# Feed-forward gate and up products: hi and lo parts of x side by side as one moving operand of 512 columns

## The chip, the cores and the metric

The kernel runs on one core of one Trainium2 chip. The metric is device time in microseconds (us), from the start to the end of one execution; the lower, the better.

## The reference, cut to what matters

A trunk of two layers (DEPTH = 2) over 256 tokens (S) of 1024 channels (D). Each layer has three token mixers, an output projection, a layer norm, a feed-forward part and a second layer norm. The change touches the first half of the feed-forward part, where `x1` is the result of the first norm:

```python
hidden = silu(einsum('bsd,df->bsf', x1, w_ffn_gate[i])) * einsum('bsd,df->bsf', x1, w_ffn_up[i])
ffn = einsum('bsf,fd->bsd', hidden, w_ffn_down[i])
```

The hidden width f is 2816, so the gate and up matrices are 1024 x 2816 each, per layer, in float32.

## The kernel before, in words

**Products.** Every float32 operand a is split into a high part ah, rounded to the matmul's operand type (fp32r), and a low part al = a - ah. A product a·b is taken as ah·bh + ah·bl + al·bh: three matmuls that add into the same PSUM columns. `mm3` (lines 246 to 250) issues these three, so lines L248, L249 and L250 carry nearly all matmul records. In a record "g<-xh,whi" the tile behind the arrow comes first that is moved through the array, then the one that is loaded into it (the stationary operand).

**Weights.** They come as one stream of pieces of 1 MB (128 x 2048 numbers): `dma_chunk` loads a piece into `raw` (three buffers), `split_chunk` makes `whi` on ScalarE (L206) and `wlo` on VectorE (L207) (three buffers each) and then starts the load of a later piece. Each step of the program ends with `step_end`, which splits one piece. At the time that a piece is used, the two behind it are split already; the split of the third behind it takes the buffers that the piece just used leaves.

**Two shapes of product.** Where the result is wanted with channels on the partitions, `gemm_cols` (L252 to L257) is used: a piece holds 256 output columns of the weights for all of the 8 k tiles; for each half m of 128 columns and each k, 128 x 128 weights are stationary and the 256 tokens of x are moved. That is 2 x 8 x 3 = 48 matmuls of 256 columns for a piece, into the two halves of one PSUM bank. Where tokens are wanted on the partitions (`gemm_tok`, `rows_gemm`), the activations are stationary and 512 columns of the weights are moved.

**Feed-forward.** For each layer, 11 rounds (L858 to L868) of a gate piece and an up piece:

```python
pg, pu = gbank(), gbank()
gemm_cols(use_chunk(), xk, pg)
s = misc([P, 2, S])
A.activation(out=s, in_=pg..., func=AF.Silu)      # L862
step_end()
gemm_cols(use_chunk(), xk, pu)
V.tensor_tensor(out=s, in0=s, in1=pu..., op=ALU.mult)   # L865
split_to(hs[...][:, 0, ...], hs[...][:, 1, ...], s)     # L288, L289
step_end()
```

So both layers use 44 pieces in this stage. Its result `hs` feeds the down projection (`rows_gemm`), whose end feeds the second norm. `xh` and `xl`, the parts of x, are two tiles of [128, 8, 256]. There are eight PSUM banks: four handed out in turn by `gbank`, four by `tbank` (transposes, attention and recurrence; unused in the feed-forward rounds).

**Order.** The instructions are placed on the engines by a scheduler; each engine then runs its own in that order, and waits on semaphores.

Of the kernel before, what the change touches and what calls it, by code (L numbers as in the profile page):

```python
# [15 lines left out]
P = 128  # L16
# [13 lines left out]

# columns of the constants' array
K_DIST = 0
# [46 lines left out]
def trunk(ctx: ExitStack, tc: tile.TileContext, x, p, w_in, pool_w, pool_scale, w_branch_a,  # L79
# [13 lines left out]
    def slot(tag, shape, dt=F32):  # L93
        return sl.tile(shape, dt, tag=tag, name=tag)
# [13 lines left out]
    def gbank():  # L108
        return psg.tile([P, 512], F32, tag="g", name="g")

    def tbank():
        return pst.tile([P, 512], F32, tag="t", name="t")
# [3 lines left out]

# [1 line left out]
    ident = cst.tile([P, P], F32, name="ident")  # L118
# [7 lines left out]

# [1 line left out]
    chunks = []  # L128
# [87 lines left out]

# [1 line left out]
    tasks = []  # L218
# [25 lines left out]

# [1 line left out]
    def mm3(ps, a, b, first, last):  # L246
# [5 lines left out]
    def gemm_cols(w, act, ps, nk=8, m0=0, nm=2):  # L252
        for m in range(nm):
            for k in range(nk):
                ms = slice((m0 + m) * P, (m0 + m + 1) * P)
                mm3(ps[:, m * S:(m + 1) * S], (w[0][:, k, ms], w[1][:, k, ms]),
                    act(k), k == 0, k == nk - 1)  # L257

    def xk(k):
        return xh[:, k, :], xl[:, k, :]  # L260
# [7 lines left out]
    def gemm_tok(ws, act, evac, between):  # L268
        """512 output columns, both tiles of tokens, ws: two pieces of four k tiles."""
        for t in range(2):  # L270
            ps = gbank()
            for k in range(KD):
                w = ws[k // 4]
                mm3(ps, act(k, t), (w[0][:, k % 4, :], w[1][:, k % 4, :]), k == 0, k == KD - 1)
                if t == 0 and k == 5 and between is not None:
                    between()
            evac(t, ps)
# [7 lines left out]
    def split_to(hi, lo, src, scale=None):  # L285
        """hi and lo parts of src (SBUF or PSUM), scaled per partition."""
        if scale is None:
            A.activation(out=hi, in_=src, func=AF.Copy)  # L288
            V.tensor_tensor(out=lo, in0=src, in1=f(hi), op=ALU.subtract)  # L289
        else:  # L290
            A.activation(out=hi, in_=src, func=AF.Copy, scale=scale)
            V.scalar_tensor_tensor(out=lo, in0=src, scalar=scale, in1=f(hi), op0=ALU.mult, op1=ALU.subtract)

# [1 line left out]
    def rsqrt(out, v, n):  # L295
# [16 lines left out]
    def layer_norm(t, gb, ress, then):  # L312
        """ress: per half of the columns (base, scale or None, psum)."""
        st = small([P, 2, 6], "ln_st")
        for hf, (base, scale, ps) in enumerate(ress):
            dst = xt[:, t, 512 * hf:512 * hf + 512]
            if scale is None:
                V.tensor_tensor(out=dst, in0=base, in1=ps, op=ALU.add)
            else:
                V.scalar_tensor_tensor(out=dst, in0=base, scalar=scale, in1=ps, op0=ALU.mult, op1=ALU.add)  # L320
            V.bn_stats(out=st[:, hf, :], in_=dst)  # L321
        mv = small([P, 2], "ln_mv")
        V.bn_aggr(out=mv, in_=st)
        ve = small([P, 1], "ln_ve")
        V.tensor_scalar(out=ve, in0=mv[:, 1:2], scalar1=LN_EPS, scalar2=None, op0=ALU.add)
        r = small([P, 1], "ln_r")
        rsqrt(r, ve, 1)
        for hf in range(2):
            cs = slice(512 * hf, 512 * hf + 512)
            V.scalar_tensor_tensor(out=xt[:, t, cs], in0=xt[:, t, cs], scalar=mv[:, 0:1], in1=gb[:, 0, cs],  # L330
                                   op0=ALU.subtract, op1=ALU.mult)
            V.scalar_tensor_tensor(out=xt[:, t, cs], in0=xt[:, t, cs], scalar=r, in1=gb[:, 1, cs],
                                   op0=ALU.mult, op1=ALU.add)
            then(t, hf)
# [6 lines left out]

# [1 line left out]
    def hgrn_task(l, hp, q, ff, kf, fb, kb, vt, gt, oh, ol):  # L343
# [14 lines left out]
        for d in range(2):  # L358
# [29 lines left out]
            yield 660  # L388
            # totals of the chunks of 32
            u = 31 if fwd else 0  # L390
# [4 lines left out]
            kb_ = range(0, 3) if fwd else range(1, 4)  # L395
            # blocks of 64 stand at 0, 2, 4; the one scaled to its tile's far end beside the middle one
            for L, blks, src, intra, own, far, fac in (
# [14 lines left out]
            V.tensor_tensor(out=t64, in0=tot[:, :, :, 0, :], in1=tot[:, :, :, 1, :], op=ALU.mult)  # L412
            # scaled: fwd queries block 3 by total of 2, keys block 0 by total of 1; bwd mirrored
            for L, lo_side, sc in ((QL, not fwd, 2 if fwd else 1), (KL, fwd, 1 if fwd else 2)):
# [14 lines left out]
            for h in range(2):  # L429
                for t in range(2):  # L430
                    # fwd: queries block 2t+1, keys block 2t; bwd: the other way
                    po = 0 if fwd else 64
                    co = (2 * h + t) * 64
                    PE.matmul(cr[po:po + 64, co:co + 64], lhsT=KL[:, h, 4 * t, :], rhs=QL[:, h, 4 * t, :],  # L434
                              start=True, stop=True)
                qp = QL[:, h, 2:4, :] if fwd else QL[:, h, 1:3, :]
                kp = KL[:, h, 1:3, :] if fwd else KL[:, h, 2:4, :]
                co = (2 * h + d) * P
                PE.matmul(lg[:, co:co + P], lhsT=kp.rearrange("p b u -> p (b u)"),  # L439
                          rhs=qp.rearrange("p b u -> p (b u)"), start=True, stop=True)  # L440
# [53 lines left out]

# [1 line left out]
    def attn_task(j, qs, ks, va, vb, ob):  # L496
# [45 lines left out]

# [1 line left out]
    def pool_task(g, a, mix):  # L544
        # a: [P, 2, 272], the channels' values between zeros
        while busy or any(t[0] == "attn1" for t in tasks):
# [7 lines left out]
        for s in range(g + 1):  # L554
            nxt = work([P, 2, 272])
            sh = 1 if s == 0 else 1 << (s - 1)
            # first step: out[t] = a[t-1] + a[t]; then out[t] = cur[t-sh] + cur[t+sh]
            l2 = lo + sh
            r2 = n if s == 0 else n - sh
            right = 0 if s == 0 else sh  # L560
            V.tensor_tensor(out=nxt[:, :, l2:r2], in0=cur[:, :, l2 - sh:r2 - sh],
                            in1=cur[:, :, l2 + right:r2 + right], op=ALU.add)
            cur, lo, n = nxt, l2, r2
            yield 620
# [14 lines left out]

# [1 line left out]
    xh, xl = slot("xh", [P, KD, S], F32R), slot("xl", [P, KD, S], F32R)  # L581
    load_x(0)
# [51 lines left out]
    for l in range(DEPTH):  # L634
        # token-major operands: the recurrence's values and gate
        vt = slot("s4", [P, 2, D])
# [18 lines left out]
        for hp in range(4):  # L655
# [26 lines left out]
            if hp < 3:  # L682
# [3 lines left out]
                tok_block(xperm, ev)  # L686
        # attention
        ob = slot("s8", [P, 2, 4, S], F32R)
# [28 lines left out]

        # gates and branches
        finish("hgrn")
# [66 lines left out]

        # output projection, first norm
        pT = slot("s7", [P, 2, S])
# [10 lines left out]
        def rows_gemm(n, late, act, base):  # L799
            """all columns of both tiles of tokens; the last pieces go tile by tile."""  # L800
            banks = [[gbank(), gbank()], [gbank(), gbank()]]
# [23 lines left out]

        xh, xl = slot("xh", [P, KD, S], F32R), slot("xl", [P, KD, S], F32R)

# [4 lines left out]

        # per-layer embedding
        pl2 = slot("s6", [P, 2, D])
# [19 lines left out]

        # feed-forward
        hs = [slot(tag, [P, 2, 4, S], F32R) for tag in ("sa", "sb", "s4", "s5", "s8")]
        hs.append(slot("s7", [P, 2, 2, S], F32R))
        for c in range(NF // 2):  # L858
            pg, pu = gbank(), gbank()
            gemm_cols(use_chunk(), xk, pg)  # L860
            s = misc([P, 2, S])
            A.activation(out=s, in_=pg.rearrange("p (m t) -> p m t", t=S), func=AF.Silu)  # L862
            step_end()
            gemm_cols(use_chunk(), xk, pu)
            V.tensor_tensor(out=s, in0=s, in1=pu.rearrange("p (m t) -> p m t", t=S), op=ALU.mult)  # L865
            i = 2 * (c % 2)
            split_to(hs[c // 2][:, 0, i:i + 2, :], hs[c // 2][:, 1, i:i + 2, :], s)
            step_end()  # L868
        gb = load_gb("s6", ln2_g[l], ln2_b[l])
        xh, xl = slot("xh", [P, KD, S], F32R), slot("xl", [P, KD, S], F32R)  # L870
        last = l == DEPTH - 1
# [47 lines left out]
```

## Time and profile before

| | |
|---|---|
| time, median of 3 runs | 1344.53 us (1342.67 to 1344.79) |
| profiled execution, first to last instruction (span) | 1341.4 us; no time of its own is listed for it beside the span |
| TensorE matmul busy | 1317.5 us (98%), 9609 matmuls |
| TensorE weight load busy | 1236.9 us (92%) |
| VectorE busy | 868.7 us (65%) |
| ScalarE busy | 585.9 us (44%) |
| mean DMA rate | 174 GB/s |
| mean granted TensorE clock | 0.997 of full speed |

Matmuls overlap in their records: the duration of one (283 ns for 256 columns) counts from its start to its modelled end, while the next starts much earlier. What a matmul costs in a row of matmuls is therefore the distance from one start to the next, which the timeline shows. PE is TensorE's matmul, PEld its weight load, DVE is VectorE, ACT ScalarE, SP the engine that issues the loads.

### The profile page before, as it was taken

The page shows a single profiled execution, that of the slowest core. Times are in us where ns is not written, and L with a number is a line of the kernel's source. Part 1 is how long each engine was busy: PE and PEld are TensorE (multiplying, and loading weights), DVE is VectorE, ACT ScalarE, POOL GpSimd, SP SyncE. Part 2 cuts the span into 40 slices and gives each one's busy share as a digit, 9 for nine tenths or more (in the row PEclk, how much of TensorE's full clock was granted, in tenths as well). Part 3 has the DMA queues.
Part 4 walks back from the last instruction along what each step waited for, and adds up shares of the span by engine and source line. Part 5 has one row for each costly group of instructions (what it writes and reads, how often), then busy time and mean ns, then how long its engine had stood idle before and what let it go on. Part 6 is the DMA issues. An engine that isn't in the chain of part 4 may idle for free.

```text
span 1341.4 us, 22091 instructions
## 1 busy us (share of the span) xinstructions
PE 1317.5 (98%) x9609; PEld 1236.9 (92%) x9609; DVE 868.7 (65%) x1126; ACT 585.9 (44%) x644; POOL 16.6 (1%) x24
## 2 busy tenths in 40 slices
PE   8999999999999999999989999999999999999997
PEld 6899999999999799998779999999999997999986
DVE  4598888574655765544555999875746558544545
ACT  5444444553444444443334444455534444444431
POOL 0000000000000000000000000000000000000000
PEclk9999999999999999999999999999999999999999
DMA  8654544245556465655356554442455564765551
GB/s 309 200 178 158 178 138 161 93 156 181 176 186 219 158 221 188 189 186 190 127 184 196 179 164 158 158 158 95 159 168 186 188 216 142 239 188 183 179 195 40
DMA packets 180769, 233.56 MB, mean 174 GB/s; under 512 B 3841, under 2 KB 149825, under 8 KB 180673
## 3 DMA queue, kind: packets, MB, share of 16 engines
q1 hardware_dynamic: 178976, 227.44, 51.7%
q10 hardware_dynamic: 1696, 4.72, 1.1%
q8 instruction: 75, 1.23, 0.4%
q14 instruction: 22, 0.17, 0.0%
HBM read 231.10 MB, written 1.05 MB: 173 GB/s over the span
## 4 chain that ended last, share of the span: by engine, by line
PE 93%; DVE 4%; issue 1%; ACT 1%; POOL 1%; DMA 0%; POOLq 0%; DVEq 0%; ACTq 0%
PE g L248 29%; PE g L249 28%; PE g L250 28%; DVE wlo L207 2%; PE t L439 1%; PE t L426 1%; PE t L434 1%; PE t L307 1%; POOL rs_y L297 1%; PE t L523 1%; PE t L463 1%; PE t L464 1%; ACT whi L206 0%; DVE ln_st L321 0%; PE t L503 0%
## 5 line engine op out<-in xcount | busy, mean ns | idle before, releaser
L207 DVE TENSOR_TENSOR wlo<-raw,whi 128x2048 fp32r<-128x2048 f32 (+2 forms) x218 | 489.9, 2248 | 339.7 <-ACT whi L206 339.4
L206 ACT ACTIVATE whi<-raw 128x2048 fp32r<-128x2048 f32 (+2 forms) x218 | 410.0, 1883 | 566.7 <-issue 259.6
L248 PE MATMUL g<-xh,whi 128*128 128x256 f32 x1984 | 564.4, 284 | 0.0
L250 PE MATMUL g<-xh,wlo 128*128 128x256 f32 x1984 | 561.7, 283 | 0.0
L249 PE MATMUL g<-xl,whi 128*128 128x256 f32 x1984 | 561.6, 283 | 0.0
L248 PEld LDWEIGHTS g<-xh,whi 128*128 128x128 f32 x1984 | 380.7, 192 | 0.2
L249 PEld LDWEIGHTS g<-xl,whi 128*128 128x128 f32 x1984 | 380.7, 192 | 0.2
L250 PEld LDWEIGHTS g<-xh,wlo 128*128 128x128 f32 x1984 | 380.6, 192 | 0.0
L248 PE MATMUL g<-whi,xh 128*128 128x512 f32 x288 | 115.1, 400 | 1.2 <-ACT whi L206 1.2
L249 PE MATMUL g<-wlo,xh 128*128 128x512 f32 x288 | 114.6, 398 | 1.4 <-DVE wlo L207 1.4
L250 PE MATMUL g<-whi,xl 128*128 128x512 f32 x288 | 113.3, 395 | 0.0
L249 PEld LDWEIGHTS g<-wlo,xh 128*128 128x128 f32 x288 | 55.6, 193 | 14.1 <-DVE wlo L207 3.1
L248 PEld LDWEIGHTS g<-whi,xh 128*128 128x128 f32 x288 | 55.6, 193 | 13.7 <-ACT whi L206 1.8
L250 PEld LDWEIGHTS g<-whi,xl 128*128 128x128 f32 x288 | 55.4, 192 | 11.5
L248 PE MATMUL g<-s,whi 128*128 128x256 f32 x192 | 54.3, 283 | 0.0
L250 PE MATMUL g<-s,wlo 128*128 128x256 f32 x192 | 54.3, 283 | 0.0
L249 PE MATMUL g<-s,whi 128*128 128x256 f32 x192 | 54.3, 283 | 0.0
L249 PE MATMUL g<-wlo,s 128*128 128x512 f32 x128 | 50.1, 392 | 0.0
L250 PE MATMUL g<-whi,s 128*128 128x512 f32 x128 | 50.1, 391 | 0.0
L248 PE MATMUL g<-whi,s 128*128 128x512 f32 x128 | 49.6, 390 | 0.0
L865 DVE TENSOR_TENSOR m<-m,g 128x512 f32<-128x512 f32 x22 | 15.1, 687 | 36.9 <-PE g L250 36.9
L248 PE MATMUL g<-whi,sa 128*128 128x512 f32 x96 | 37.5, 391 | 0.0
(177 smaller groups left out, 1472.4 us busy)
## 6 DMA issues: line engine op xcount, KB each, us to landing
raw<-in_w_in_dram SPq DMA_DIRECT2D x106, 1024.0 KB, 5.1
raw<-in_w_ffn_gate_dram SPq DMA_DIRECT2D x22, 1024.0 KB, 5.4
raw<-in_w_ffn_up_dram SPq DMA_DIRECT2D x22, 1024.0 KB, 5.4
raw<-in_w_ffn_down_dram SPq DMA_DIRECT2D x22, 1024.0 KB, 4.8
raw<-in_w_branch_c_dram SPq DMA_DIRECT2D x8, 1024.0 KB, 5.0
raw<-in_w_branch_a_dram SPq DMA_DIRECT2D x8, 1024.0 KB, 5.0
raw<-in_w_out_dram SPq DMA_DIRECT2D x8, 1024.0 KB, 4.8
raw<-in_w_ple_gate_dram SPq DMA_DIRECT2D x8, 1024.0 KB, 5.1
```

The costliest lines, as they stand in the source:

```text
L206: A.activation(out=hi[:, ks, :], in_=t[:, ks, :], func=AF.Copy)
L207: V.tensor_tensor(out=lo[:, ks, :], in0=t[:, ks, :], in1=f(hi[:, ks, :]), op=ALU.subtract)
L248: PE.matmul(ps, lhsT=ah, rhs=bh, start=first, stop=False)
L249: PE.matmul(ps, lhsT=ah, rhs=bl, start=False, stop=False)
L250: PE.matmul(ps, lhsT=al, rhs=bh, start=False, stop=last)
L297: G.tensor_tensor(out=y, in0=v, in1=mhalf.to_broadcast([P, n]) if n > 1 else mhalf, op=ALU.pow)
L307: PE.transpose(ps[:, k * P:(k + 1) * P], xt[:, t, (4 * hf + k) * P:(4 * hf + k + 1) * P], ident)
L426: PE.matmul(dg[po:po + 64, co:co + 64], lhsT=KI[:, cs], rhs=QI[:, cs], start=True, stop=True)
L434: PE.matmul(cr[po:po + 64, co:co + 64], lhsT=KL[:, h, 4 * t, :], rhs=QL[:, h, 4 * t, :], start=True, stop=True)
L439: PE.matmul(lg[:, co:co + P], lhsT=kp.rearrange("p b u -> p (b u)"), rhs=qp.rearrange("p b u -> p (b u)"), start=True, stop=True)
L463: PE.matmul(o, lhsT=at[:, 2 * h + t, :], rhs=vt[:, t, hs], start=True, stop=False)
L865: V.tensor_tensor(out=s, in0=s, in1=pu.rearrange("p (m t) -> p m t", t=S), op=ALU.mult)
```

## The change

In the feed-forward rounds, `gemm_cols` is replaced by `gemm_wide`. The tiles `xh` and `xl` become the two halves of one tile `xx` of [128, 8, 2, 256], so that for a k tile hi and lo parts of x lie side by side as 512 columns; `xh` and `xl` stay as names of the halves for all other products. For each half m and each k the weights' high part is loaded once and all 512 columns are moved (this gives whi·xh in columns 0 to 255 of a bank and whi·xl in columns 256 to 511); the weights' low part is loaded and the 256 columns of xh are moved, added into columns 0 to 255. So two matmuls (one of 512 columns, "wide", one of 256, "narrow") stand for three of 256. One bank now holds one half m, so that a piece takes two banks: gate pieces take them from `gbank`, up pieces from `tbank`. `joined` reads them: ScalarE copies the first half of the bank to SBUF, VectorE adds the second half, once for each m. Silu and the product of gate and up then read SBUF.

```diff
+    def gemm_wide(w, ps):
+        for m in range(2):
+            ms = slice(m * P, (m + 1) * P)
+            for k in range(KD):
+                wide = (ps[m], w[0][:, k, ms], xx[:, k].rearrange("p a t -> p (a t)"))
+                narrow = (ps[m][:, 0:S], w[1][:, k, ms], xx[:, k, 0, :])
+                for i, (o, a, b) in enumerate((wide, narrow) if k == 0 else (narrow, wide)):
+                    PE.matmul(o, lhsT=a, rhs=b, start=k == 0 and i == 0, stop=k == KD - 1 and i == 1,
+                              skip_group_check=True)
+
+    def joined(ps, dst):
+        for m in range(2):
+            A.activation(out=dst[:, m, :], in_=ps[m][:, 0:S], func=AF.Copy)
+            V.tensor_tensor(out=dst[:, m, :], in0=dst[:, m, :], in1=ps[m][:, S:2 * S], op=ALU.add)
...
-    xh, xl = slot("xh", [P, KD, S], F32R), slot("xl", [P, KD, S], F32R)
+    xx = slot("xx", [P, KD, 2, S], F32R)
+    xh, xl = xx[:, :, 0, :], xx[:, :, 1, :]
...
         for c in range(NF // 2):
-            pg, pu = gbank(), gbank()
-            gemm_cols(use_chunk(), xk, pg)
-            s = misc([P, 2, S])
-            A.activation(out=s, in_=pg.rearrange("p (m t) -> p m t", t=S), func=AF.Silu)
+            pg, pu = [gbank(), gbank()], [tbank(), tbank()]
+            gemm_wide(use_chunk(), pg)
+            s, u = misc([P, 2, S]), misc([P, 2, S])
+            joined(pg, s)
+            A.activation(out=s, in_=s, func=AF.Silu)
             step_end()
-            gemm_cols(use_chunk(), xk, pu)
-            V.tensor_tensor(out=s, in0=s, in1=pu.rearrange("p (m t) -> p m t", t=S), op=ALU.mult)
+            gemm_wide(use_chunk(), pu)
+            joined(pu, u)
+            V.tensor_tensor(out=s, in0=s, in1=u, op=ALU.mult)
             i = 2 * (c % 2)
             split_to(hs[c // 2][:, 0, i:i + 2, :], hs[c // 2][:, 1, i:i + 2, :], s)
             step_end()
```

In the changed file the matmuls of `gemm_wide` are on L268, the copy and the addition of `joined` on L274 and L275, Silu on L883, the product of gate and up on L887, and the lines 288 and 289 of before are 306 and 307.

TensorE's order at the first gate piece of layer 0, before (g is a PSUM bank; a name in brackets is a semaphore that the instruction waits for):

```order
L248 MATMUL g<-xh,whi 128x256 [waits Activation_49]
L249 MATMUL g<-xl,whi 128x256
L250 MATMUL g<-xh,wlo 128x256 [waits DVE_49]
L248 MATMUL g<-xh,whi 128x256
L249 MATMUL g<-xl,whi 128x256
L250 MATMUL g<-xh,wlo 128x256
```

The same place in the changed kernel:

```order
L268 MATMUL g<-xx,whi 128x512 [waits Activation_49]
L268 MATMUL g<-xx,wlo 128x256 [waits DVE_49]
L268 MATMUL g<-xx,wlo 128x256
L268 MATMUL g<-xx,whi 128x512
L268 MATMUL g<-xx,wlo 128x256
L268 MATMUL g<-xx,whi 128x512
L268 MATMUL g<-xx,wlo 128x256
```

Three narrow matmuls became one wide and one narrow, which alternate from the second k on; outside of the feed-forward rounds the order of TensorE, and that of the other engines and of the loads, is that of before.

ScalarE's order in one round of a gate piece and an up piece (the third round of layer 0), before; `whi` is the split of a later piece, the last row the high part of hidden:

```order
L206 ACTIVATE whi<-raw 128x2048 [waits DMAHW2_49,PE_49,Activation_49]
L862 ACTIVATE m<-g 128x512 [waits PE_49]
L206 ACTIVATE whi<-raw 128x2048 [waits DMAHW3_49,PE_49,Activation_49]
L288 ACTIVATE sb<-m 128x512 [waits DVE_49]
```

The same round in the changed kernel:

```order
L274 ACTIVATE m<-g 128x256 [waits PE_49] x2
L206 ACTIVATE whi<-raw 128x2048 [waits DMAHW2_49,Activation_49]
L883 ACTIVATE m<-m 128x512 [waits DVE_49]
L274 ACTIVATE m<-t 128x256 [waits PE_49,Activation_49]
L274 ACTIVATE m<-t 128x256 [waits PE_49]
L206 ACTIVATE whi<-raw 128x2048 [waits DMAHW3_49,Activation_49]
L306 ACTIVATE sb<-m 128x512 [waits DVE_49]
```

The two copies of a piece's halves now stand ahead of the split of a later piece, and Silu waits for VectorE's additions instead of for TensorE.

VectorE's order from a split to the low part of hidden, in a round of layer 0, before:

```order
L207 TENSOR_TENSOR wlo<-raw,whi 128x2048 [waits DMAHW4_49,PE_49,Activation_49]
L865 TENSOR_TENSOR m<-m,g 128x512 [waits PE_49,Activation_49]
L207 TENSOR_TENSOR wlo<-raw,whi 128x2048 [waits DMAHW5_49,Activation_49]
L289 TENSOR_TENSOR sb<-m,sb 128x512 [waits Activation_49]
```

The same round in the changed kernel:

```order
L275 TENSOR_TENSOR m<-m,g 128x256 [waits Activation_49] x2
L207 TENSOR_TENSOR wlo<-raw,whi 128x2048 [waits DMAHW4_49,Activation_49]
L275 TENSOR_TENSOR m<-m,t 128x256 [waits Activation_49] x2
L887 TENSOR_TENSOR m<-m 128x512 [waits DVE_49]
L207 TENSOR_TENSOR wlo<-raw,whi 128x2048 [waits DMAHW5_49,Activation_49]
L307 TENSOR_TENSOR sb<-m,sb 128x512 [waits Activation_49]
```

Two additions stand ahead of each split, each of which waits for ScalarE's copy.

## Rows read from the trace of the kernel before

**Rows 1.** The page: the chain that ended last, shares of the span by engine.

```profile
PE 93%; DVE 4%; issue 1%; ACT 1%; POOL 1%; DMA 0%; POOLq 0%; DVEq 0%; ACTq 0%
```

**Rows 2.** Busy times by stretch: both feed-forward stages, then a row of wide matmuls.

```profile
core 0: us, PE busy (x) PEld busy (x) DVE busy (x) ACT busy (x) POOL busy (x), PEclk, DMA share, GB/s
480.07:606.78 126.71, 126.71 (x1057) 126.70 (x1056) 66.24 (x45) 54.51 (x45) 0.00 (x0) 1.00 0.60 192
1145.98:1272.70 126.72, 126.72 (x1058) 126.71 (x1056) 66.24 (x45) 54.49 (x45) 0.00 (x0) 1.00 0.60 192
608.17:617.69 9.52, 9.52 (x43) 7.88 (x42) 5.19 (x3) 3.09 (x3) 0.00 (x0) 1.00 0.48 179
```

**Rows 3.** Timeline of PE where the stage begins: start, duration, engine, line, out<-in.

```profile
479.62 0.39 PE L249 MATMUL g<-wlo,xh 128*128 128x512 f32 x1
479.85 0.39 PE L250 MATMUL g<-whi,xl 128*128 128x512 f32 x1
480.07 0.28 PE L248 MATMUL g<-xh,whi 128*128 128x256 f32 x1
480.19 0.28 PE L249 MATMUL g<-xl,whi 128*128 128x256 f32 x1
```

**Rows 4.** Timeline of PE where the stage ends and the down projection begins.

```profile
606.66 0.28 PE L250 MATMUL g<-xh,wlo 128*128 128x256 f32 x1
606.78 0.40 PE L248 MATMUL g<-whi,sa 128*128 128x512 f32 x1
607.02 0.40 PE L249 MATMUL g<-wlo,sa 128*128 128x512 f32 x1
...
608.17 0.39 PE L248 MATMUL g<-whi,sa 128*128 128x512 f32 x1
```

**Rows 5.** Waits of PE: who waited for whom, us in total, times, longest.

```profile
PE t L307 <- DVE x L332: 7.5, 6, 3.5
PE t L307 <- DMA x<-in_x_dram: 3.7, 1, 3.7
PE g L249 <- DVE wlo L207: 1.4, 1, 1.4
```

**Rows 6.** Groups by shape: busy us, mean ns of one, idle time before them.

```profile
L698 ACT ACTIVATE h<-g 128x256 f32<-128x256 f32 x48 | 15.5, 378 | 6.0 <-DVE w L406 6.0
L865 DVE TENSOR_TENSOR m<-m,g 128x512 f32<-128x512 f32 x22 | 15.1, 687 | 36.9 <-PE g L250 36.9
L383 DVE TENSOR_TENSOR w<-h,w 128x256 f32<-128x256 f32 x16 | 6.6, 415 | 3.2 <-PE t L426 3.2
```

**Rows 7.** Timelines of ACT, then DVE, then SP, over the first pieces of the stage.

```profile
485.95 1.92 ACT L206 ACTIVATE whi<-raw 128x2048 fp32r<-128x2048 f32 x1 [3.28 <-PE g L249]
...
487.90 2.29 DVE L207 TENSOR_TENSOR wlo<-raw,whi 128x2048 fp32r<-128x2048 f32 x1 [2.58 <-ACT whi L206]
...
490.22 0.37 SPq L193 DMA_DIRECT2D raw<-in_w_ffn_gate_dram  x1
```

**Rows 8.** The page: DMA issues, KB each, us from issue to landing.

```profile
raw<-in_w_ffn_gate_dram SPq DMA_DIRECT2D x22, 1024.0 KB, 5.4
```

**Rows 9.** Timeline of PE behind the second norm of layer 0, then that stretch's busy times.

```profile
679.25 1.33 PE L307 MATMUL t<-ident,x 128*128 128x128 f32 x8 [3.47 <-DVE x L332]
...
681.19 0.63 PE L249 MATMUL g<-wlo,xh 128*128 128x512 f32 x1
681.62 0.63 PE L248 MATMUL g<-whi,xh 128*128 128x512 f32 x1
...
683.75 0.44 PE L250 MATMUL g<-whi,xl 128*128 128x512 f32 x1
...
680.00:690.00 10.00, 9.98 (x39) 7.96 (x40) 3.65 (x3) 4.72 (x5) 0.00 (x0) 0.83 0.03 10
```

More of the change, by code (lines that the diff above doesn't have):

```diff
@@ L824, in rows_gemm @@
                 step_end()
-        xh, xl = slot("xh", [P, KD, S], F32R), slot("xl", [P, KD, S], F32R)
+        xx = slot("xx", [P, KD, 2, S], F32R)
+        xh, xl = xx[:, :, 0, :], xx[:, :, 1, :]
         def ln1(t, b):
@@ L869, in trunk @@
         gb = load_gb("s6", ln2_g[l], ln2_b[l])
-        xh, xl = slot("xh", [P, KD, S], F32R), slot("xl", [P, KD, S], F32R)
+        xx = slot("xx", [P, KD, 2, S], F32R)
+        xh, xl = xx[:, :, 0, :], xx[:, :, 1, :]
         last = l == DEPTH - 1
```

## The prediction

> **What bounds the kernel now.** I read four views, from the whole to the place. First the chain that ended last [rows 1]: TensorE (PE) holds 93% of it, so a stage in which PE never waits is worth exactly what PE's own work in it shrinks by. Second the waits of PE [rows 5]: what PE waits for are transposes behind a norm (L307), the first load of x, and one or two splits; none of the matmuls of the feed-forward rounds is named as waiting. Third the busy times by stretch [rows 2]: in both feed-forward stages, 126.71 and 126.72 us long, PE is busy for all of it, while VectorE has 66 us of work and ScalarE 54.5. So this stage is PE and nothing else, and the other two have half of it free. Fourth the timeline, for the distance from one matmul's start to the next, which is what a matmul costs in a row of them; its recorded duration of 0.28 us is more than twice that.
>
> Two such distances carry the whole sum. A stage is 22 pieces of 48 narrow matmuls (256 columns), 1056 in all, as the count of weight loads (PEld) says; the count of PE has one or two more that still run in from outside: 126.71 / 1056 = 0.1200 us each [rows 2]. The nearest long run of wide matmuls (512 columns) is the down projection: from 608.17 to 617.69 there are 42 of them, counted by weight loads: 9.52 / 42 = 0.2267 us each [rows 2]. Twice the columns cost 0.1067 us more. If 256 columns cost 0.1067 us, a narrow matmul has 0.1200 - 0.1067 = 0.0133 us that does not depend on its columns, and so has a wide one. I call that the start of a matmul.
>
> **The change, part by part.** *Matmuls.* For each half and each k, three narrow ones (0.3600 us) become one wide and one narrow (0.2267 + 0.1200 = 0.3467). The columns are the same 768; what goes is one start, 0.0133 us. A piece has 2 x 8 such places, both layers have 44 pieces: 704 starts x 0.0133 = 9.4 us, or 4.7 us a stage, which should come down from 126.7 to 122.0. All of it lies on the chain.
>
> The row says 0.0133 us for a start. The Trainium skill, page "TensorE: Matmul & The Clock Gate", section "Back-to-back issue gap", gives N/2.4 + 2.5 ns for a lone stream at full clock, so only 2.5 ns that do not depend on the columns; by it my estimate for the saving would be 704 x 2.5 ns = 1.8 us, which nobody could measure here. By that formula the two distances would be 109 and 216 ns; the trace has 120.0 and 226.7, so here the trace disagrees with the page, and I take the rows.
>
> *Reading the banks.* Each piece gains two copies of 128x256 on ScalarE and two additions of 128x256 on VectorE. The nearest rows: a ScalarE instruction of that shape from PSUM takes 0.378 us (L698); for the addition the ends are 0.415 us (L383, same shape, no PSUM) and half of L865's 0.687, 0.344 us (half the columns, from PSUM) [rows 6]. I take 0.415, since a short instruction is not half of a long one. Silu and the product keep their shape and read SBUF; I leave their price. That makes 22 x 0.76 = 16.6 us more on ScalarE, 54.5 + 16.6 = 71 of 122 us, and 22 x 0.83 = 18.3 us more on VectorE, 66.2 + 18.3 = 84.5 of 122 us. Both stay below the stage's length, so I cost them at nothing; without that cover they would be 17 or 18 us a layer.
>
> *What is queued behind the new instructions.* Each engine runs in order, so the split of a later piece now stands behind the copies. A piece that starts at 480.07 ends 48 x 0.12 later, at 485.83; its split partner (the third piece behind it) begins on ScalarE at 485.95, on VectorE at 487.90, and is done at 490.19 [rows 7], 4.4 us after the piece's end. The copy of the second half puts 0.38 us ahead of it; VectorE's addition runs beside the split on ScalarE and adds nothing. So it is done 4.7 us after the piece's end, and PE wants it only two pieces later, after 2 x 5.55 = 11.1 us: 6.4 us to spare. Silu now waits for VectorE's second addition, but that is done (0.38 + 0.42 us) while ScalarE is still in the split ahead of it. The load that is issued at 490.22 [rows 7], when the split ends, lands after 5.4 us [rows 8], and its own split comes three pieces behind the first, 16.6 us after 485.95, at 502.6 in place of 503.2: 7 us to spare. SP's queue is as before.
>
> *Banks.* A bank is written anew after four pieces (eight halves in eight banks), some 22 us; its readers are done within a piece's length. Nothing. What was held up behind the stage, the down projection, takes other banks than the last piece's and uses the last part of hidden at its very end. Nothing.
>
> *Layout of x.* The split of x behind a norm writes with twice the distance between k tiles, and the other products read the same runs of x as before. Ends: nothing, or a few ns for each of the few writes. Nothing.
>
> **The sum** against the profiled execution: 1341.4 - 9.4 = 1332.0 us of span. The median of the runs is 3.1 us above that span (the lowest run 1.3); I let that distance stand, so 1344.5 - 9.4 = 1335.1 us.
>
> **The rivals.** *A wide matmul behind a narrow one costs more than in a row of its kind.* Where the narrow run ends, the first wide one takes 0.24 us to the next start, and the six from 606.78 to 608.17 take 1.39 us where six of 0.2267 take 1.36 [rows 4]: 0.005 us each. Now every wide one follows a narrow one. With 0.005 on each, 704 x 0.005 = 3.5 us are lost again: 1338.6. Against it stands the other joint: from the last wide start before the stage to the second narrow one are 0.34 us [rows 3] where 0.2267 + 0.1200 are 0.3467, so that the two joints may cancel. Chance 0.09.
>
> *Only that second joint holds*: 0.0067 us less for each pair, 704 x 0.0067 = 4.7 us more gain: 1330.4. Chance 0.04.
>
> *The distance goes by what is loaded, not by the width.* The wide rows that I read have activations loaded and weights moved; in the changed stage it is the other way round, as in the narrow rows. And in the narrow stage the weight load (PEld) is busy for 126.70 of 126.71 us, against 7.88 of 9.52 in the wide stretch [rows 2]. If each column of this stage costs 0.1200 / 256 us whatever the width, a wide one takes 0.24 us and nothing is gained: 1344.5. For it: the load is as full as PE. Against it: both kinds load 128x128, and the two distances differ by 256 columns at one rate. Chance 0.05.
>
> *Slower: each change of width costs the whole settling.* The six wide starts behind the narrow run lose 0.03 us in all [rows 4]. If that is the price of one change of width, and is paid at once each time, 704 x 0.03 = 21.1 us come on, against 9.4 saved: 1356.2. It decides from 0.0133 us a pair on. Against it: the first wide one shows at most 0.0133 of it, and the joint of rows 3 shows no loss. Chance 0.04.
>
> That the change does not do what it says I leave out: the new order of TensorE has one wide and one narrow for every three.
>
> **How the numbers follow.** My forecast, the plain sum, has 0.78. Its own width: the runs lie from 1.9 below to 0.3 above the median; and behind the second norm of layer 0, where PE had waited 3.47 us, the starts of wide ones stand 0.43 us apart, six in 2.56 us from 681.19 to 683.75 [rows 9]. The granted clock there is 0.83 in a stretch of 10 us, which is half speed (1.2 in place of 2.4 GHz) for about 3.4 us, worth 1.7 us. Whether that happens once, twice or not at all may change when the stages shift by 4.7 us. Together 1331.5 to 1337.1; to hold 8 in 10 with the first rival's 1338.6 inside it, 1331.5 to 1339.0. Left out are the fall to 1330.4, no change and slower, 0.13.
>
> A difference of 0.2% (2.7 us) is about what a measurement of this kernel can tell from none. Faster by more: the forecast, the first and the second rival, 0.78 + 0.09 + 0.04 = 0.91. Within it: the third, 0.05. Slower: 0.04.
>
> **What will show it.** Right, if the trace of the changed kernel has 8905 matmuls, both stages at 122.0 us with PE busy throughout, 0.347 us from one wide start to the next, no wait of PE on L268, and VectorE at some 85 us in a stage. If the stage is longer with PE full, it is one of the joints, and the distances behind wide and narrow ones say which. If PE has gaps at L268, the splits or the banks are late and my spare time of 6.4 us was wrong. If the stage has 122 us and the time does not follow, it was given back behind a norm.

## The result and the profile after

The changed kernel takes 1336.74 us (median of 4 runs, 1335.85 to 1337.37), against 1343.68 us before (median of 4 runs, 1342.67 to 1344.79, the three shown above and one more beside the new kernel). The ratio is 0.9948, with a 95% interval from 0.9936 to 0.9960: 0.4% to 0.6% faster. The forecast was 1335.1 us, faster, within 1331.5 to 1339.0; the time lies inside, and 6.9 us were saved where 9.4 were forecast.

The busy times of the changed kernel in both feed-forward stages, and then in a stretch behind the second norm of layer 0 (columns as in [rows 2]):

```profile
480.69:603.73 123.04, 123.04 (x705) 107.21 (x704) 82.43 (x88) 69.04 (x88) 0.00 (x0) 1.00 0.62 197
1143.82:1266.87 123.05, 123.05 (x705) 107.21 (x704) 82.44 (x88) 68.97 (x88) 0.00 (x0) 1.00 0.62 197
676.29:681.64 5.35, 5.35 (x16) 4.34 (x17) 1.90 (x3) 1.20 (x2) 0.00 (x0) 0.50 0.17 64
```

The stages went from 126.71 and 126.72 us [rows 2] to 123.04 and 123.05, 3.67 each, where the forecast said 4.7. PE is busy for all of it, as before. The trace has 8905 matmuls, as forecast. The weight load, whose row had been as full as PE's, now has 16 us free in a stage; but the record of one load lasts 0.19 us, so this row is full wherever loads start closer together than that, and by itself it says little about a limit.

The waits of PE in the changed kernel:

```profile
PE t L325 <- DVE x L350: 7.6, 6, 3.6
PE t L325 <- DMA x<-in_x_dram: 3.7, 1, 3.7
PE g L249 <- DVE wlo L207: 1.4, 1, 1.4
```

They are those of [rows 5], one for one; no matmul of L268 is among them. So nothing holds PE up in the stage: its own matmuls take longer than forecast. Its timeline, in the first half of an up piece, shows where:

```profile
486.74 0.40 PE L268 MATMUL t<-xx,whi 128*128 128x512 f32 x1
486.97 0.28 PE L268 MATMUL t<-xx,wlo 128*128 128x256 f32 x1
487.09 0.40 PE L268 MATMUL t<-xx,whi 128*128 128x512 f32 x1
487.33 0.28 PE L268 MATMUL t<-xx,wlo 128*128 128x256 f32 x1
487.45 0.40 PE L268 MATMUL t<-xx,whi 128*128 128x512 f32 x1
487.69 0.28 PE L268 MATMUL t<-xx,wlo 128*128 128x256 f32 x1
487.80 0.40 PE L268 MATMUL t<-xx,whi 128*128 128x512 f32 x1
```

A wide start is followed after 0.23 to 0.24 us, a narrow one after 0.11 to 0.12. Over the whole stage of layer 0, read to the nanosecond, a wide one takes 233.8 ns on average (7.2 more than 226.7) and a narrow one 115.8 (4.2 less than 120.0). Over a stage, a pair takes 123.05 / 352 = 0.3496 us where 0.2267 + 0.1200 = 0.3467 were forecast. The excess is not even: by the starts in the trace, the eight pairs of the first half of a piece take 352.1 ns each, those of the second half 347.1, in piece after piece.

The new readers, in the groups by shape:

```profile
L275 DVE TENSOR_TENSOR m<-m,g 128x256 f32<-128x256 f32 x44 | 18.4, 418 | 12.4 <-ACT m L274 12.4
L274 ACT ACTIVATE m<-t 128x256 f32<-128x256 f32 x44 | 16.9, 384 | 52.4 <-PE t L268 52.2
```

**Where the span went.** From 1341.4 to 1335.6 us it fell by 5.8 in these two profiled executions. The two stages give 7.3. Two other stretches, whose order of work is the same in both kernels, give some back. The stage of layer 0 begins at 480.69 in place of 480.07, 0.6 us later. From its end to the stage of layer 1 there are 1143.82 - 603.73 = 540.09 us, where there were 1145.98 - 606.78 = 539.20, 0.9 more. The second is the clock behind the norm. In the timeline of the changed kernel, after the wait for the norm:

```profile
676.29 1.94 PE L325 MATMUL t<-ident,x 128*128 128x128 f32 x8 [3.58 <-DVE x L350]
...
678.65 0.63 PE L249 MATMUL g<-wlo,xx 128*128 128x512 f32 x1
...
681.64 0.58 PE L248 MATMUL g<-whi,xx 128*128 128x512 f32 x1
682.06 0.40 PE L249 MATMUL g<-wlo,xx 128*128 128x512 f32 x1
```

The steps of 0.43 us (half speed, 1.2 in place of 2.4 GHz; the row above has a granted clock of 0.50 there) last from 678.65 to 682.06, eight of them, where before there were six, from 681.19 to 683.75 [rows 9], and the transposes ahead of them already take 1.94 us in place of 1.33. This comes with the run and not with the change: the four runs of the changed kernel itself have spans of 1334.1 and 1334.5 us with a mean granted clock of 0.997, and of 1335.4 and 1335.6 with 0.996. Likewise, from the end of one stage to the start of the other there are 539.2 to 539.4 us in the profiled runs of before and of e1, e2, e4 and e9 below, and 539.8 to 540.3 us in those of the changed kernel and of e3, e5, e6, e7 and e11, while the program between the stages does the same in all of them.

The 0.6 us at the start are of the same kind. In the changed kernel, the first products run at half speed up to a start at 12.96:

```profile
12.53 0.63 PE L248 MATMUL g<-whi,xx 128*128 128x512 f32 x1
12.96 0.43 PE L249 MATMUL g<-wlo,xx 128*128 128x512 f32 x1
```

The next start is at 13.23. Before, the last of these steps of 0.43 ended at 11.20. (The windows of the profile list a granted clock of 1.00 for this stretch in both, so here the half speed is read from the steps alone.) In the other kernels below whose part ahead of the stage is the same (all but e8 and e10), the stage of layer 0 begins anywhere from 479.68 to 480.64, so this too comes with the run and not with the change.

### The profile page after: what moved, and what is told of

It reads as the page before. It is cut to its first block, busy times and chain, and to the rows that moved or that the text cites. A ratio compares the mean times of both kernels' runs of the same rounds, so it can differ in the third digit from the quotient of the medians.

```text
span 1335.6 us, 20897 instructions
## 1 busy us (share of the span) xinstructions
PE 1311.6 (98%) x8905; PEld 1199.4 (90%) x8905; DVE 902.0 (68%) x1214; ACT 615.1 (46%) x732; POOL 16.7 (1%) x24
## 4 chain that ended last, share of the span: by engine, by line
PE 93%; DVE 4%; issue 1%; ACT 1%; POOL 1%; DMA 0%; POOLq 0%; DVEq 0%; ACTq 0%
PE g L248 22%; PE g L249 22%; PE g L250 22%; PE t L268 9%; PE g L268 9%; DVE wlo L207 2%; PE t L457 1%; PE t L444 1%; PE t L452 1%; PE t L325 1%; POOL rs_y L315 1%; PE t L541 1%; PE t L481 1%; PE t L482 1%; ACT whi L206 0%
## 5 line engine op out<-in xcount | busy, mean ns | idle before, releaser
L248 PE MATMUL g<-xx,whi 128*128 128x256 f32 x1280 | 365.2, 285 | 0.0
L250 PE MATMUL g<-xx,wlo 128*128 128x256 f32 x1280 | 362.5, 283 | 0.0
L249 PE MATMUL g<-xx,whi 128*128 128x256 f32 x1280 | 362.4, 283 | 0.0
L248 PEld LDWEIGHTS g<-xx,whi 128*128 128x128 f32 x1280 | 245.6, 192 | 0.2
L249 PEld LDWEIGHTS g<-xx,whi 128*128 128x128 f32 x1280 | 245.6, 192 | 0.2
L250 PEld LDWEIGHTS g<-xx,wlo 128*128 128x128 f32 x1280 | 245.5, 192 | 0.0
L268 PE MATMUL t<-xx,whi 128*128 128x512 f32 x352 | 123.6, 396 | 0.0
L268 PE MATMUL g<-xx,whi 128*128 128x512 f32 x352 | 123.6, 396 | 0.0
L248 PE MATMUL g<-whi,xx 128*128 128x512 f32 x288 | 115.7, 402 | 1.2 <-ACT whi L206 1.2
L249 PE MATMUL g<-wlo,xx 128*128 128x512 f32 x288 | 114.8, 398 | 1.4 <-DVE wlo L207 1.4
L250 PE MATMUL g<-whi,xx 128*128 128x512 f32 x288 | 113.6, 396 | 0.0
L268 PE MATMUL g<-xx,wlo 128*128 128x256 f32 x352 | 90.9, 279 | 0.0
L268 PE MATMUL t<-xx,wlo 128*128 128x256 f32 x352 | 90.9, 279 | 0.0
L268 PEld LDWEIGHTS g<-xx,whi 128*128 128x128 f32 x352 | 64.5, 188 | 12.0
L268 PEld LDWEIGHTS t<-xx,whi 128*128 128x128 f32 x352 | 64.5, 188 | 11.9
L268 PEld LDWEIGHTS t<-xx,wlo 128*128 128x128 f32 x352 | 66.3, 188 | 3.9
L268 PEld LDWEIGHTS g<-xx,wlo 128*128 128x128 f32 x352 | 66.3, 188 | 3.9
L248 PEld LDWEIGHTS g<-whi,xx 128*128 128x128 f32 x288 | 55.9, 194 | 13.7 <-ACT whi L206 1.8
L250 PEld LDWEIGHTS g<-whi,xx 128*128 128x128 f32 x288 | 55.6, 193 | 11.7
```

The source lines that it names most:

```text
L248: PE.matmul(ps, lhsT=ah, rhs=bh, start=first, stop=False)
L249: PE.matmul(ps, lhsT=ah, rhs=bl, start=False, stop=False)
L250: PE.matmul(ps, lhsT=al, rhs=bh, start=False, stop=last)
L268: PE.matmul(o, lhsT=a, rhs=b, start=k == 0 and i == 0, stop=k == KD - 1 and i == 1, skip_group_check=True)
```

## The experiments

Eleven kernels ran. The question was why a pair takes 2.9 ns more than the sum of its parts, and whether the readers, the layout, the halves or the banks have a share in it. The stage is compared by its length in the trace, which is the same in both layers to 0.02 us in every kernel; a kernel's single time carries the run's clock with it.

**e1_grouped: in each half the wide ones first, then the narrow ones.**

```diff
-            for k in range(KD):
...
-                for i, (o, a, b) in enumerate((wide, narrow) if k == 0 else (narrow, wide)):
...
+            wide = [(ps[m], w[0][:, k, ms], xx[:, k].rearrange("p a t -> p (a t)")) for k in range(KD)]
+            narrow = [(ps[m][:, 0:S], w[1][:, k, ms], xx[:, k, 0, :]) for k in range(KD)]
+            order = wide + narrow
+            for i, (o, a, b) in enumerate(order):
...
```

> For each half the eight wide matmuls come first, then the eight narrow ones; nothing else differs from the changed kernel, whose feed-forward stage takes 123.05 us (a wide and a narrow one together 349.6 ns on average, 352.0 in the first half of a piece and 347.1 in the second). Theory 'joints' (the step between a wide and a narrow one costs 2.9 ns a pair): with two joints left in a half instead of sixteen, a pair costs 226.7 + 120.0 = 346.7 ns and the stage 122.0 to 122.2 us. Theory 'first half' (something of the first half of a piece, its weights' place, its bank or its time, costs 5 ns a pair): the stage stays at 123.0 us and the first half at 352.

Measured: 1336.06 us (median of 4; ratio to before 0.9948, interval 0.9932 to 0.9965), stage 122.88 us. Its timeline, merged by group:

```profile
490.82 2.00 PE L268 MATMUL g<-xx,whi 128*128 128x512 f32 x8
492.67 1.11 PE L268 MATMUL g<-xx,wlo 128*128 128x256 f32 x8
493.62 2.00 PE L268 MATMUL g<-xx,whi 128*128 128x512 f32 x8
```

Eight wide ones take 1.84 to 1.85 us from first start to the next group, where 8 x 0.2267 = 1.81; eight narrow ones 0.95, where 8 x 0.1200 = 0.96. By the single starts: behind a narrow run, wide ones step by 233, 236, 229, 232, 231 and then 227 ns, 27.7 ns over in all; behind a wide run, narrow ones step by 113, 119 and then 120, 8 ns under. That is 19.7 ns a trip (from narrow to wide and back), or 2.5 ns a pair here. The first half is no longer slower than the second (349.0 and 349.2). Neither expectation met it: the joints do not vanish, because the whole price of a joint is spread over several matmuls, and where the widths alternate the next joint comes before it is paid. A stage of the changed kernel has 308 such trips and is 1.03 us over 352 undisturbed pairs (122.02 us): 3.3 ns a trip. This run has 44, and 0.86 us over: 19.5 ns a trip.

**e2_halves_swapped** (`for m in (1, 0)`), **e3_banks_swapped** (`ps[1 - m]` in place of `ps[m]`, in the products and in the join).

> The loop over the two halves of a piece runs backwards (columns 128 to 255 of the weights first), each with the bank that it had. Theory 'place': the half with columns 0 to 127 costs 352 ns a pair wherever it comes, so now the second in time. Theory 'time': the first in time costs 352, whichever columns it has (it runs while ScalarE and VectorE split the next piece). Both: the stage at 123.0 us. Theory 'joints' says nothing of the halves.

> The two halves of a piece exchange their PSUM banks, and the readers with them; columns and order stay. Theory 'bank': the first half falls to 347 ns a pair and the second rises to 352. Theories 'place' and 'time': the first stays at 352, the second at 347. The stage at 123.0 us in each.

Measured: 1336.05 and 1336.84 us (one run each). The stage is 123.05 us in both, and in both it is the half that comes first in time that takes 352.1 ns a pair, the second 347.1. So neither the weights' columns nor the bank matter. In the first half the steps repeat after three k (117 and 241, 120 and 236, 113 and 233), in the second after two (118 and 231, 112 and 233).

**e4_wnnw: wide, narrow, narrow, wide in turn** (shown against e1).

```diff
-            order = wide + narrow
+            order = [x for k in range(KD) for x in ((wide[k], narrow[k]) if k % 2 == 0 else (narrow[k], wide[k]))]
```

> Wide, narrow, narrow, wide in turn: half as many changes of width as in the changed kernel. Theory 'joints': half of the 2.9 ns a pair goes, the stage takes 122.5 us. Theory 'first half': 123.0 us, as in the changed kernel.

Measured: 1334.78 us (one run), stage 122.61 us, 348.3 ns a pair in both halves. There are 176 trips in a stage in place of 308 (a little over half), and they leave 1.6 of the 2.9 ns: 3.3 ns a trip, as in the changed kernel.

**e9_one_trip_a_piece: 16 wide ones, then 16 narrow ones.**

> For each piece all 16 wide matmuls first, then all 16 narrow ones. In the grouped run eight wide ones behind a narrow one took 1841 ns (27.7 more than 8 x 226.7) and eight narrow ones behind a wide one 952 (8 less than 8 x 120.0): 19.7 ns for each trip from narrow to wide and back. Theory 'settling' (that price is paid once a trip, however long the runs are): one trip a piece in place of two, 22 x (5547 + 19.7) ns = 122.5 us for the stage. Theory 'width alone' (the excess belongs to the wide ones and not to the change): 122.9 us as in the grouped run.

Measured: 1334.60 us (one run).

```profile
479.87:602.31 122.44, 122.44 (x706) 108.24 (x704) 80.29 (x87) 67.47 (x87) 0.00 (x0) 1.00 0.63 202
```

The stage is 122.44 us where 122.5 were expected: the price is one of the change of width, 19 to 20 ns for a trip once the runs are long enough, and not one of each wide matmul.

**e11_all_wide: the narrow one made wide** (it adds the product of both low parts, which the kernel does without).

```diff
-                narrow = (ps[m][:, 0:S], w[1][:, k, ms], xx[:, k, 0, :])
+                narrow = (ps[m], w[1][:, k, ms], xx[:, k].rearrange("p a t -> p (a t)"))
```

> The narrow matmul is made wide too (the weights' low part also moves the low part of x, one product more than the kernel needs), so that no change of width is left. Theory 'width' (a wide matmul costs 226.7 ns whichever operand is moved): 704 x 226.7 ns = 159.6 us a stage, and a span some 36.5 us longer than that of the changed kernel, near 1408. Theory 'what is loaded' (with the weights loaded a wide one costs 240 ns): 169 us a stage.

Measured: 1410.14 us (one run).

```profile
480.27:639.84 159.57, 159.57 (x705) 132.18 (x704) 82.45 (x88) 69.08 (x88) 0.00 (x0) 1.00 0.48 154
```

159.57 / 704 = 0.2267 us, to the last digit the step of the down projection [rows 2]. So a wide matmul costs the same whichever operand is loaded, and without a change of width no settling shows.

**e6_half_columns: in the rounds of before, the second and third of each three move 128 columns** (half of the correction terms is left out). Its three matmuls, with `o` the half of the bank, and one of the two calls:

```diff
+                PE.matmul(o, lhsT=w[0][:, k, ms], rhs=xh[:, k, :], start=k == 0, stop=False)
+                PE.matmul(o[:, 0:P], lhsT=w[0][:, k, ms], rhs=xl[:, k, 0:P], start=False, stop=False)
+                PE.matmul(o[:, 0:P], lhsT=w[1][:, k, ms], rhs=xh[:, k, 0:P], start=False, stop=k == KD - 1)
...
-            gemm_cols(use_chunk(), xk, pg)
+            gemm_half(use_chunk(), pg)
```

> The kernel before, but in the feed-forward rounds the second and third matmul of each three move 128 columns (half of the tokens) in place of 256: half of the correction terms is left out. Theory 'start' (a matmul costs 0.417 ns a column and 13.3 ns that do not depend on columns): 120.0 + 2 x 66.7 = 253.3 ns for three, the stage 89.2 us. Theory 'load' (a narrow matmul's 120 ns is the time that the next weights take to be loaded): three still cost 360 ns and the stage 126.7 us, or little less.

Measured: 1330.34 us (one run).

```profile
480.64:600.27 119.63, 119.63 (x1058) 119.63 (x1056) 66.23 (x45) 54.50 (x45) 0.00 (x0) 1.00 0.63 203
```

A third of the columns is gone, and the stage falls by 7.1 us only, not by 37.5. Three matmuls take 119.63 / 352 = 0.3399 us, 113.3 ns each on average: theory 'start' fell, and 'load' came nearer without being met (340 ns for three, not 360). That the row of the weight load is full does not decide it, since it is as full before, at 120.0 ns. The distance between starts tells more. Two loads from the timeline:

```profile
519.97 0.19 PEld L264 LDWEIGHTS g<-xh,whi 128*128 128x128 f32 x1
520.08 0.19 PEld L265 LDWEIGHTS g<-xl,whi 128*128 128x128 f32 x1
```

All through the stage the loads start 107 to 122 ns apart, 113.3 on average, while the matmuls step by 168 ns behind one of 256 columns and by 59 and 113 behind the two of 128. So a single matmul of 128 columns can be followed after 59 ns, and it is the nearly even loads that look like the floor. This run changes widths too; but the dearest change that the other runs show, 20 ns there and back, is small against the 87 ns that three matmuls take beyond theory 'start'. The Trainium skill, page "TensorE: Matmul & The Clock Gate", section "LDWEIGHTS (loading the stationary operand)", gives P/1.2 ns for P columns, which makes an estimate of 106.7 for 128. The loads here start 107 to 122 ns apart, so the trace agrees with it at the lower end and is 7 ns over it on average.

**e5_layout_alone** (x side by side, rounds as before) and **e7_join_doubled** (each join done twice).

> x lies as in the changed kernel (hi and lo side by side in one tile), but the feed-forward rounds are those of before: three narrow matmuls, one bank a piece, no join. Theory 'the layout is free': stage 126.7 us, span within 1 us of the 1341.4 of before. Theory 'the layout costs': the 2.9 ns a pair that are missing come from reading x in its new place, so the stage of narrow matmuls grows too, by about 1 us, to 127.7.

> The changed kernel with the join of each piece done a second time, into a tile that nobody reads: two more copies on ScalarE and two more additions on VectorE for each piece. Theory 'the readers are hidden': VectorE goes from 84 to about 102 us in a stage and the stage stays at 123.05 us, with no wait of PE. Theory 'the readers hold PE up a little': the 1 us that the stage is longer than forecast doubles, to 124.1 us or more.

Measured: 1344.42 and 1336.59 us (one run each). With the layout alone the stage is 126.71 us, that of before; its span, 1342.6, is 1.2 us over that of before, a little more than expected, with the stage starting at 480.64 and a mean clock of 0.995 (0.997 before); other runs of before have spans from 1340.7 to 1343.0. With the join doubled:

```profile
480.25:603.30 123.05, 123.05 (x706) 107.21 (x705) 94.89 (x130) 78.29 (x130) 0.00 (x0) 1.00 0.62 197
```

VectorE has 95 us of work (102 were expected; back to back, the records of 0.41 us start 0.33 us apart), ScalarE 78, and the stage is 123.05 us as without. The layout is free, and the readers are hidden with room for as much again.

**e8_gates_too and e10_attention_too: more pieces with wide products.** e8 has the order of e4 and takes the 8 gate pieces of each layer whose product follows at once; e10 also takes attention's 12 pieces and pooling's 4. Of the new lines, the first five are in both, the last three in e10 alone (for attention).

```diff
+            pw = [gbank(), gbank()]
+            gemm_wide(use_chunk(), pw)
+            s = misc([P, 512])
+            joined(pw, s.rearrange("p (m t) -> p m t", t=S))
+            A.activation(out=s, in_=s, func=AF.Tanh, scale=0.5)
...
+                    A.activation(out=o, in_=pw[h][:, 0:S].rearrange(...), func=AF.Copy, scale=sc)
+                    V.scalar_tensor_tensor(out=o, in0=pw[h][:, S:2 * S].rearrange(...),
+                                           scalar=sc, in1=o, op0=ALU.mult, op1=ALU.add)
```

> Wide, narrow, narrow, wide in the feed-forward rounds, and the same wide products and join for 8 of the gate pieces of each layer (those whose product follows them at once), 16 pieces more. By 'joints', each piece saves 48 x 120.0 - 16 x 348.3 = 187 ns: 3.0 us less than the wide-narrow-narrow-wide run, a span near 1330 and a time near 1331.8. Rival 'VectorE is too full there': the gate rounds share VectorE with attention and pooling, PE waits for a bank or a split, and the gain is lost.

> The gates-too run, and wide products also for the 12 pieces of attention's queries and keys and the 4 of pooling in each layer, 32 pieces more; there the join goes into the readers that are there anyway (VectorE adds the second half onto what ScalarE wrote). At the 0.17 us that a gate piece saved, 32 x 0.17 = 5.4 us less than the gates-too run: a time near 1327. Rival 'banks': a piece now takes two of four banks, so a reader that is late by one piece holds PE up; with VectorE and ScalarE full of attention and recurrence, PE waits for readers and the gain is lost.

Measured: e8 1332.63 us (one run), e10 1327.04 us (median of 4, 1326.32 to 1327.63), a ratio of 0.9881 to the kernel before, interval 0.9864 to 0.9897. In e8, one of the gate pieces that became wide:

```profile
380.22:385.81 5.59, 5.59 (x35) 4.88 (x33) 3.56 (x4) 2.79 (x3) 0.00 (x0) 1.00 0.57 187
```

It takes 5.59 us, where 48 narrow ones take 48 x 0.1200 = 5.76. The expected 3.0 us came out as 2.1 in the spans (1333.0 in e4, 1330.9 in e8). Start against start, e8's work ran 1.13 us behind that of e4 once the first products had left half speed (up to a start at 12.36, in e4 up to about 11): from a lead of 0.2 it lost 0.7 us at a second wait of PE for the load of x at the very start, and 0.6 by the half speed. It kept that to the first gate piece. Then each wide gate piece brought 0.17 to 0.19 us, and behind the eighth e8 was 0.29 ahead: 1.4 us for the layer, and 1.4 again in the second; another 0.4 came from the half speed behind the norm between them. So the pieces brought 2.8 of the 3.0 us, and the late start hid part of it. e10 then met its forecast near 1327. Start against start, its 32 further pieces brought 2.7 us in each layer over e8, 5.4 in all as forecast; the spans of the two profiled runs (1330.9 and 1324.5) lie 6.3 us apart, mostly because e10 did not have e8's late start. PE waits there for what it waits for in [rows 5] and for nothing else that is longer than 1.2 us, so two banks a piece are enough. It beats both kernels.

## Why the prediction held, and where it was off

*The bound.* Right. PE fills the stage before and after, no wait came in its place, and the time fell because the stages did.

*The sum.* The term that was mis-sized is "one wide and one narrow (0.2267 + 0.1200 = 0.3467)". Both paces are right in a run of their kind: e9 has 0.120 for narrow ones once they have settled and 0.2267 for wide ones, e11 has 0.2267 throughout. Alternating, the pair costs 0.3496. So 10.4 of the 13.3 ns are saved each time, 704 x 10.4 ns = 7.3 us where 9.4 were forecast. Both the first and the second rival had a part of the mechanism: a wide matmul behind a narrow one costs more (7.2 ns where the first rival said 5), and a narrow one behind a wide one costs less (4.2 ns where the second said 6.7). The prediction took them for alternatives, or for a pair that may cancel; they come together, and 2.9 ns are left.

*The start of a matmul*, 13.3 ns that do not depend on the columns, fits the two widths that it was taken from, which is all that the forecast needed; two widths cannot show that it is a constant. Below 256 columns it does not hold: e6 takes 113.3 ns a matmul on average, at the pace of the weight loads, just under the 120.0 of a narrow one.

*What is loaded.* The third rival fell with e11: the width sets the price, not the role. Its support, a weight load as full as PE, was a weak sign: the records of 0.19 us overlap at every step below that, and e6 shows the loads going at 113.3 ns with a row no fuller.

*Slower.* The whole settling, 19 to 20 ns for a trip there and back rather than 30, is paid only when the runs on both sides are long (e1, e9). Alternating pays 3.3 ns a trip, 2.9 a pair.

*Readers, queue and banks.* Costed at nothing, rightly (e7, and no wait of PE on L268). ScalarE's copy takes 384 ns (378 forecast), VectorE's addition 418 (415); the sums in a stage are 69.0 and 82.4 us (71 and 84.5 forecast). The split that follows the first gate piece is done 4.7 us after that piece's end, as forecast: the piece ends at 486.27, and VectorE's split runs from 488.69 for 2.29 us, as its timeline shows.

```profile
488.69 2.29 DVE L207 TENSOR_TENSOR wlo<-raw,whi 128x2048 fp32r<-128x2048 f32 x1 [1.39 <-ACT whi L206]
```

*The layout of x.* Free (e5).

*The distance from span to time*, 3.1 us, was wrong, and it hid part of the miss. In every run whose time and span are both on record the time is 1.7 to 1.9 us above the span (1337.37 and 1335.6 for the profiled run of the changed kernel); 3.1 came of setting the median of three runs against the span of another. The span was forecast at 1332.0 and measured at 1335.6, 3.6 over. The time is only 1.6 over, since 1.3 us of this went into the distance and 0.6 is what the median of four runs lies below the profiled one. So the forecast of the time came out closer than its working deserved, and that part is luck. The pairs (2.1 us), the start of the stage (0.6) and the clock behind the norm (0.9) make up the 3.6 us; the range had room for them. The median of before, too, came down by 0.85 us with the fourth run.

**What stays open.** Why the first matmuls behind a change of width step by other amounts, and why in the changed kernel the half that comes first in time settles into the dearer rhythm. e2 and e3 rule out the columns and the bank, and with twice the joins (e7) the halves still take 352.1 and 347.1 ns. In e4 both openings of the halves (steps of 231, 113, 119, 233 and of 236, 116, 112, 233 ns) follow each other in turn inside every half, so nothing of a half as such is needed for them. That the weight load stands near its floor in a narrow run (e6) and not in a wide one suits it, but no run separates that. That the loads are the floor in e6 is likewise read from the trace and not tested. The cause of the later rise of the clock in some runs was not tried either.

## What to carry to other kernels

In a stage that one engine fills, take prices from the distance between starts, not from durations, and take them from a run with the same mix: two paces from uniform runs left out 2.9 ns a pair here, a fifth of the gain. One wide moving operand saves a start for each pair of matmuls with the same weights, and is worth having where the engines that join the halves have time to spare. Fewer changes of width are worth a little more, but not in proportion to their number (a stage takes 123.05 us as changed, 122.88 with eight of a kind in a row, 122.61 with two, 122.44 with sixteen), and more pieces treated so are worth most (1327.04 us for the kernel). The distance between time and span has to come from one and the same run.

## What the runs showed of the hardware that was not expected

Fewer columns brought little: with 128 in place of 256 in two of three matmuls, a stage fell from 126.71 to 119.63 us, to 113.3 ns a matmul on average, with loads that start 107 to 122 ns apart. A change between 256 and 512 columns costs 19 to 20 ns there and back where the runs are long (e1, e9), spread over the seven matmuls behind the two changes, and 3.3 ns where the widths alternate by one or two (the changed kernel, e4). And the point at which the first products leave half speed differs from run to run (a start at 11.20 us in the profile of before, at 12.96 in that of the changed kernel); with it the whole program shifts by up to a microsecond, 479.68 to 480.69 at the stage of layer 0, which is as much as some of the effects looked for.
